# Down projection of a SwiGLU block as seven half-block products, with accumulation over two row pairs

## The chip, the core and the metric

The kernel runs on one NeuronCore of one Trainium2 chip. The metric is the device time of one execution in microseconds (us); the median of three runs before the change is 2986.15 us (2983.44 to 2987.88).

## The reference

One inference step of one decoder layer, all in float32, for a prompt of 2048 tokens and 8 decode tokens that share the weights (model width 1024). A mixer (Conformer convolution beside gated DeltaNet) with one output projection, attention into 256 memory tokens, and the dense network which the change is about:

```python
def swiglu(h, w_gate, w_up, w_down):
    return (jax.nn.silu(h @ w_gate) * (h @ w_up)) @ w_down

    x = x + y
    x = x + memory_attend(rms_norm(x, norm_mem_q), mem_k, mem_v, w_mq, w_mo)
    x = x + swiglu(rms_norm(x, norm_ffn), w_gate, w_up, w_down)
```

`w_gate` and `w_up` are 1024 x 2816, `w_down` is 2816 x 1024. A final RMS norm gives the outputs.

## The kernel before, in words

Everything is held transposed: channels on the 128 partitions, tokens along the free axis. The prompt is cut into NB = 4 blocks of TB = 512 tokens. Block 2 (`DEC_F`) carries the 8 decode tokens through the dense network, so its half blocks are 260 wide, not 256 (`width`).

**Precision.** Each float32 operand is split into a high part (a rounded float32r copy made by ScalarE) and a low part (the difference, formed on GpSimd or VectorE). `three` issues three matmuls for a product: high x high, high x low, low x high. A weight tile `w` of 128 x 2 x 512 holds both parts of four 128x128 weights. `WS` brings weights in: `load` fills a `raw` tile by DMA, `split` makes the `w` tile from it. There are NRAW = 11 raw tiles and NW = 6 weight tiles. `plan` lists them in the order of use.

**Gate and up.** The 2816 columns are NF = 22 column tiles f. For each, the two projections are computed together on half blocks of tokens in seven products, Q1, P5, P6, Q2, Q3, Q7, P4, by the Strassen-Winograd scheme: each is 4 x 3 matmuls of 256 (260) columns into one of the accumulators fx, fy, fz. Between products VectorE or ScalarE reads the accumulator and TensorE then adds the next product to it. Four of the seven weight tiles are sums of weight blocks; they are formed once (for some f in the mixer stage, for the others in block 0) and stored, split, in the DRAM tensor `sums`; later blocks load them as `w<-sums`.

**Down.** `ff_split` makes silu(gate) x up, and its two parts, for each f. Two neighbouring f are a row pair; there are NG = 11. `down(g, j)` multiplies row pair g into the two output column tiles m = 2j and 2j + 1: 2 x 2 x 3 matmuls of 512 columns (in block 2, two spans of 260 each) into a fresh PSUM bank `dn` per m. VectorE adds each bank to the residual tile `xs[m]`, and in block 2 the few decode columns into a tile `xd` of their own (`add_half`). `ffn_steps(b)` writes out the order of the steps in a block: row pair g comes in around the P4 of an even f. In block 2 the last HOLD = 3 row pairs are held back and run behind the block (`rest`), while VectorE prepares the normed operands of block 3. In block 3 `last` computes the last row pair in two spans of 256 tokens.

**Who sets the order.** The program order runs against a simple clock, in which "lanes" (generators such as `ff_split`, `ffn_norm`, `finish_x`) wait for tiles or free buffers: 28 tiles of the pool `t2`, 22 operand tiles (`act`), of which a block's normed input takes 14. All instructions are recorded on a tape; `Tape.order` then schedules the tape with a list scheduler and modelled costs and writes out the queue of every engine, TensorE's included. Each instruction therefore carries the line L469 in the profile, and is told apart by the tiles it works on. All DMAs go through the sync engine's queue. The dense networks lie at about 1290 to 1650 us (block 0), 1775 to 2130 (block 1), 2280 to 2630 (block 2), 2630 to 2965 (block 3), with the mixer's output projection and attention of blocks 2 and 3 between the first three.

Of the kernel before, what the change touches and what calls it, by code (L numbers as in the profile page):

```python
# [14 lines left out]
P = 128  # L15
# [30 lines left out]
NG = NF // 2  # L46

# [544 lines left out]
def hybrid_step(ctx: ExitStack, tc: tile.TileContext, i: dict, o: list):  # L592
# [183 lines left out]
    def ffn_steps(b):  # L776

        steps = [("Q1", 0)]
# [22 lines left out]


# [8 lines left out]
    def ffn_plan(b):  # L811
        at = {}
        for st, f, *j in ffn_steps(b):
            if st == "down":
                plan.append(("w_down", "d", f, j[0]))
            elif st == "dec":
# [70 lines left out]
    for b in range(NB):  # L887
        ffn_plan(b)
        if b + 2 < NB:
            out_plan(b + 2)  # L890
            att_plan(b + 2)
        elif b + 1 < NB:
            plan.extend(("w_down", "d", g, j) for g in range(NG - HOLD, NG) for j in range(KC // 2))
# [4 lines left out]
    class WS:  # L898
# [28 lines left out]
        def load(self):  # L927
# [4 lines left out]
            if how == "sum":  # L932
                x, y, f, k = what
                self.engine(2600.0).tensor_tensor(out=r, in0=self.raw[x], in1=self.raw[y], op=ALU.add)
                self.used(x)
                self.used(y)
            else:
                w, kind, a, b_ = what
                src = wsrc[w]
                if kind in "cd":  # L940
                    dma(r, src[a, b_], fr)
                elif kind == "q":
# [8 lines left out]
        def split(self):  # L951
# [9 lines left out]
            r = self.raw[k]  # L961
            A.activation(out=t[:, 0, :], in_=r, func=AF.Copy)
# [13 lines left out]

        def ready(self, k):
            return k < 0 or k < self.ld and C.when([self.raw[k]]) <= S.vt
# [1000 lines left out]
    wsrc["sums"] = dram.tile([NF, 4, P, 2, TB], F32, tag="sums", name="sums")  # L1979
    xpark = dram.tile([NB - 1, KC, P, TB], F32, tag="xpark", name="xpark")  # L1980
# [576 lines left out]
    def ffn_norm(b, done, op, may):  # L2557
# [10 lines left out]
        if b:  # L2568
            for k in range(KC):
                yield ("t2", 1 + RES)  # L2570
                xs[k] = t2("x")
                dma(xs[k], xpark[b - 1, k])
        if b == DEC_F:
            yield lambda: dec_lanes["f"][0] is None

# [5 lines left out]
        for k in range(4):  # L2581
            yield ("t2", 4)
            xn = []
            for kc in (k, k + 4):
                x = t2("xn", (P, 520))
                V.scalar_tensor_tensor(
                    out=halves(x, w, TB // 2), in0=halves(xs[kc], TB // 2), scalar=vcol("norm_ffn", kc),
# [38 lines left out]
    def ffn(b, op, go_on):  # L2626
# [4 lines left out]
        bank = {}  # L2631
# [13 lines left out]
        def product(st, f):  # L2645
# [31 lines left out]
            else:  # L2677
                V.tensor_tensor(out=u0, in0=pt, in1=u0, op=ALU.subtract)
                S.add(ff_split(f, u[:, : 2 * w], s_[:, : 2 * w]))
# [15 lines left out]
        def add_half(m, pts):  # L2695
            for n_, pt in enumerate(pts):
                lo, hi = n_ * TB // 2, (n_ + 1) * TB // 2
                V.tensor_tensor(out=xs[m][:, lo:hi], in0=pt[:, : TB // 2], in1=xs[m][:, lo:hi], op=ALU.add)
                if w > TB // 2:
                    dx = xd[:, m, n_ * DEC // 2 : (n_ + 1) * DEC // 2]  # L2700
                    V.tensor_tensor(out=dx, in0=pt[:, TB // 2 :], in1=dx, op=ALU.add)

        def down(g, j):
# [4 lines left out]
            for m in (2 * j, 2 * j + 1):  # L2708
                pts = [pm("dn", (P, hi - lo)) for lo, hi in spans]
                for n_, f in enumerate(fs):  # L2710
                    at = 2 * (m % 2) + n_
                    three(pts, wk(wt, 0, at), wk(wt, 1, at), hact[f], spans, n_ == 0, n_ == 1)
                    tick()
                if m % 2:
                    ws.free(1)
                if b == DEC_F:
                    add_half(m, pts)
# [7 lines left out]
        def rest():  # L2725
            for g in range(NG - HOLD, NG):
                for j in range(KC // 2):
                    down(g, j)
# [3 lines left out]
        def last():  # L2732
# [3 lines left out]
            for lo, hi in tail:  # L2736
                for m in range(KC):
                    pt = pm("dn", (P, hi - lo), ["s"])
                    for n_, f in enumerate(fs):
                        at = 2 * (m % 2) + n_  # L2740
                        three([pt], wk([wts[m // 2]], 0, at), wk([wts[m // 2]], 1, at), hact[f], [(lo, hi)], n_ == 0, n_ == 1)
# [6 lines left out]
        for st, f, *j in ffn_steps(b):  # L2748
            if st == "down":
                down(f, j[0])  # L2750
            elif st == "dec":
# [67 lines left out]
def lay_out(inp):  # L2819
# [33 lines left out]
    wd = inp["w_down"][0].reshape(NG, 2, P, KC // 2, 2, P)  # L2853
    out["w_down"] = wd.transpose(0, 3, 2, 4, 1, 5).reshape(NG, KC // 2, P, TB)
# [35 lines left out]
```

## Time and profile before

| | |
|---|---|
| median of 3 runs | 2986.15 us |
| profiled execution: time, span | 2990.62 us, 2988.8 us |
| TensorE busy, granted clock | 2932.8 us (98%), 0.994 |
| VectorE, ScalarE, GpSimd busy | 2002.1, 1312.1, 1478.9 us |
| matmuls of the down products (dn) | 2688, of these 1536 of 512 columns, 1056 of 260, 96 of 256 |
| DMA | 593.89 MB, 199 GB/s over the span |

A line of the groups reads: line, engine, operation, tile written <- tiles read, shapes, count; busy time and mean length of one; idle time of the engine just ahead of them and what ended it. Matmuls overlap, so the mean length of one is not the time that it costs; that is read from the distance of starts.

### The profile page before, as it was taken

The numbers are of one execution on the slowest core, as the hardware profiler recorded it, in microseconds if no ns is written. First come the engines' busy times: TensorE is split into PE (matmuls) and PEld (weight loads), VectorE is DVE, ScalarE is ACT, GpSimd is POOL, SyncE is SP. The second block draws the span as 40 slices with busy tenths as digits, with TensorE's granted clock in tenths as the row PEclk, the third lists the DMA queues.
The fourth block names the chain that finished last, engine by engine and source line by source line (L and its number), as shares of the span: only waits on it lengthen the run. The fifth ranks groups of instructions, "written<-read, shape, count | busy, mean of one in ns | idle before, by whom it ended". The sixth has DMA issues, their size and how long they took to land. (4 is left out here: it accounts for less than half of the span.)

```text
span 2988.8 us, 53327 instructions
## 1 busy us (share of the span) xinstructions
PE 2932.8 (98%) x18972; PEld 2609.6 (87%) x18972; DVE 2002.1 (67%) x4105; ACT 1312.1 (44%) x2672; POOL 1478.9 (49%) x1403
## 2 busy tenths in 40 slices
PE   9999999999999999999999999999999999999998
PEld 7998878887888887899988789988888999999997
DVE  8758897987755757998788974433675444664345
ACT  6533455444654344545544553333453233333233
POOL 3544554786554654457776124445413444344444
PEclk9999999999999999999999999999999999999999
DMA  6533425777663425766768767867526666666664
GB/s 213 157 102 99 138 93 173 256 236 249 222 222 117 131 82 195 234 196 212 268 252 268 247 216 244 268 220 241 185 91 227 208 226 215 212 239 220 216 224 136
DMA packets 361963, 593.89 MB, mean 199 GB/s; under 512 B 54017, under 2 KB 148545, under 8 KB 361681
## 3 DMA queue, kind: packets, MB, share of 16 engines
q1 hardware_dynamic: 361696, 590.47, 59.9%
q8 instruction: 151, 2.47, 0.3%
q14 instruction: 116, 0.94, 0.1%
HBM read 476.65 MB, written 114.27 MB: 198 GB/s over the span
## 5 line engine op out<-in xcount | busy, mean ns | idle before, releaser
L469 POOL TENSOR_TENSOR w<-raw,w 128x512 fp32r<-128x512 f32 x713 | 962.3, 1359 | 891.1 <-ACT w L469 842.3
L469 ACT ACTIVATE w<-raw 128x512 fp32r<-128x512 f32 x912 | 569.7, 631 | 905.2 <-PE fx L469 183.7
L469 PE MATMUL dn<-ff,w 128*128 128x512 f32 (+2 forms) x2688 | 518.1, 348 | 3.9 <-ACT ffs L469 2.6
L469 PEld LDWEIGHTS dn<-ff,w 128*128 128x128 f32 x2688 | 422.1, 188 | 64.7 <-ACT ffs L469 2.8
L469 PE MATMUL fy<-op,w 128*128 128x256 f32 (+1 forms) x3168 | 428.5, 283 | 4.7 <-DMA w<-sums 3.2
L469 PEld LDWEIGHTS fy<-op,w 128*128 128x128 f32 x3168 | 400.5, 189 | 10.4 <-DVE ffu L469 3.0
L469 PE MATMUL hd<-hT,w 128*128 128x512 f32 (+2 forms) x1920 | 396.7, 358 | 9.1 <-ACT w L469 5.9
L469 DVE SCALAR_TENSOR_TENSOR cacc<-cu,cw,cacc 128x512 f32<-128x512 f32 x480 | 358.2, 746 | 9.0 <-ACT cacc L469 3.8
L469 PEld LDWEIGHTS hd<-hT,w 128*128 128x128 f32 x1920 | 306.3, 190 | 54.6 <-ACT w L469 6.6
L469 DVE TENSOR_TENSOR x<-dn,x 128x512 f32<-128x512 f32 (+1 forms) x448 | 254.1, 571 | 129.2 <-PE dn L469 126.3
L469 PE MATMUL fz<-op,w 128*128 128x256 f32 (+1 forms) x2112 | 287.0, 283 | 1.0 <-DMA w<-sums 0.9
L469 PE MATMUL fx<-op,w 128*128 128x256 f32 (+1 forms) x2112 | 285.3, 283 | 1.0 <-DVE ffs L469 0.9
L469 PEld LDWEIGHTS fx<-op,w 128*128 128x128 f32 x2112 | 268.3, 189 | 7.8 <-issue 1.2
L469 PEld LDWEIGHTS fz<-op,w 128*128 128x128 f32 x2112 | 265.8, 189 | 3.7 <-issue 2.6
L469 POOL TENSOR_TENSOR sqj<-sqj,sqj 128x512 f32<-128x512 f32 (+1 forms) x98 | 134.9, 1376 | 255.7 <-ACT sqj L469 253.3
L469 DVE TENSOR_TENSOR w<-raw,w 128x512 fp32r<-128x512 f32 x199 | 167.2, 845 | 59.8 <-ACT w L469 55.8
L469 PE MATMUL sc<-w,hT 128*128 128x512 f32 x768 | 190.2, 399 | 3.2 <-DVE w L469 1.7
L469 PE MATMUL rg<-catS,w 128*128 128x512 f32 (+2 forms) x960 | 189.4, 353 | 0.0
L469 PE MATMUL rg<-pT,w 128*128 128x512 f32 x768 | 188.9, 399 | 0.4 <-ACT pT L469 0.4
L469 DVE TENSOR_TENSOR ffu<-fy,ffu 128x256 f32<-128x256 f32 (+1 forms) x176 | 74.3, 422 | 164.1 <-PE fy L469 163.7
L469 PEld LDWEIGHTS rg<-catS,w 128*128 128x128 f32 x960 | 154.4, 188 | 24.4 <-ACT jn L469 0.2
L469 PEld LDWEIGHTS sc<-w,hT 128*128 128x128 f32 x768 | 141.6, 188 | 37.5 <-DVE w L469 2.6
(378 smaller groups left out, 4089.6 us busy)
## 6 DMA issues: line engine op xcount, KB each, us to landing
w<-sums SPq DMA_DIRECT2D x296, 512.0 KB, 4.4
raw<-in_w_gate_dram SPq DMA_DIRECT2D x192, 256.0 KB, 3.2
sums<-w SPq DMA_DIRECT2D x88, 512.0 KB, 4.1
raw<-in_w_down_dram SPq DMA_DIRECT2D x176, 256.0 KB, 3.3
raw<-in_w_up_dram SPq DMA_DIRECT2D x118, 256.0 KB, 3.0
raw<-in_w_in_dram SPq DMA_DIRECT2D x96, 256.0 KB, 3.0
raw<-in_w_out_dram SPq DMA_DIRECT2D x64, 256.0 KB, 3.1
raw<-wk SPq DMA_DIRECT2D x64, 256.0 KB, 2.8
```

The lines of the kernel that those rows point to most:

```text
L469: fn(*args, **kw)
```

## The change

In blocks 1 to 3 the down products of the first 20 of the 22 column tiles f, thus of ten row pairs, are done by the same seven-product scheme. For one row pair the weight blocks are the four 128x128 blocks of two rows f and of two column tiles j and j + 4; the activations are the two rows f times the two half blocks of tokens. `downs(g, j)` takes the row pairs 2g and 2g + 1 together: each of the seven products is accumulated over both pairs (2 x 3 matmuls of 256 or 260 columns), and read by VectorE into the residual, in the order of accumulators x, y, z, x, z, x, x. The accumulators x and z go on accumulating after they have been read.

- `pair_split` replaces `ff_split` for these f: the product, four differences of half tiles on VectorE, then high and low parts in four operand tiles per row pair.
- `downs_plan`, `split_down`, `sums_down`: in block 1 the weights come as two half tiles for each row pair and j; four sums of 128x128 blocks are formed in the free halves and both tiles (512 and 384 columns) are stored unsplit in the DRAM tensor `dsums`. Blocks 2 and 3 load these. All blocks split them at each use.
- `ffn_steps_ds`: the four j of a group g stand around the P4 of two successive f (`DS_AT`). In block 2 the last group and the last row pair run in `rest`.
- The residual tiles of block 2 are 520 wide and carry the decode columns beside each half; only the last row pair writes them to `xd`.
- `down` (block 0, and the last row pair of all) takes the column tiles j and j + 4 instead of 2j and 2j + 1; the host lays `w_down` out for that.

```diff
+DS_B = 1
+NDS = 5
+
+DS_AT = ((1, 0), (1, 1), (2, 0), (2, 1))
...
+    def ffn_steps_ds(b):
...
+            units = [[], []]
+            for g in range(NDS - (b == NB - 2)):
+                for j, (df, end) in enumerate(DS_AT):
+                    if f == min(4 * g + 4 + df, NF - 1):
+                        units[end].append(("downs", g, j))
+            early = not units[0] + units[1] and f + 1 < NF
+            if early:
+                steps.append(("Q1", f + 1))
+            steps += units[0] + [("P4", f)] + units[1]
+        if b < NB - 2:
+            steps += [("down", NG - 1, j) for j in range(KC // 2)]
...
+        def sums_down(self, at, r0, r1):
+
+            (a11, a12, s1, s2), (s3, s4, a22, a21) = ([r[:, n * P : (n + 1) * P] for n in range(4)] for r in (r0, r1))
+            eng = self.engine(2600.0)
+            for out, x, y, op in (
+                (s1, a21, a22, ALU.add), (s2, s1, a11, ALU.subtract), (s3, a11, a21, ALU.subtract), (s4, a12, s2, ALU.subtract)
+            ):
+                eng.tensor_tensor(out=out, in0=x, in1=y, op=op)
+            p, j = at
+            dma(wsrc["dsums"][p, j, 0], r0)
+            dma(wsrc["dsums"][p, j, 1, :, : 3 * P], r1[:, : 3 * P])
...
+        def pair_split(p):
+
+            (u1, s1), (u2, s2) = prod.pop(2 * p), prod.pop(2 * p + 1)
+            half = lambda t, n: t[:, n * w : (n + 1) * w]
+            yield [u2, s2]
+            V.tensor_tensor(out=u2, in0=u2, in1=s2, op=ALU.mult)
+            V.tensor_tensor(out=half(s2, 1), in0=half(u2, 1), in1=half(u1, 1), op=ALU.subtract)
+            V.tensor_tensor(out=half(u1, 1), in0=half(u1, 1), in1=half(u1, 0), op=ALU.subtract)
+            V.tensor_tensor(out=half(s2, 0), in0=half(u2, 1), in1=half(u1, 1), op=ALU.subtract)
+            V.tensor_tensor(out=half(s1, 0), in0=half(u2, 0), in1=half(s2, 0), op=ALU.subtract)
+            for n, (src, wd) in enumerate(((u1, 2 * w), (u2, 2 * w), (s2, 2 * w), (s1, w))):
+                yield ("act", 1)
+                a = act("fo")
+                A.activation(out=a[:, 0, :wd], in_=src[:, :wd], func=AF.Copy)
+                yield a
+                V.tensor_tensor(out=a[:, 1, :wd], in0=src[:, :wd], in1=a[:, 0, :wd].bitcast(F32), op=ALU.subtract)
+                drop(src)
+                hx[p, n] = a
...
+        def downs(g, j):
+
+            ps_ = (2 * g, 2 * g + 1)
+            S.until(lambda: all((p, n) in hx for p in ps_ for n in range(4)), "ff")
+            wts, bk = {}, {}
+            for n, at, (x, h), t, m, half in (
+                (0, 0, (0, 0), "x", j, 0), (0, 1, (1, 0), "y", j, 0), (0, 2, (0, 1), "z", j + 4, 1), (0, 3, (2, 0), "x", j, 1),
+                (1, 1, (1, 1), "z", j, 1), (1, 0, (2, 1), "x", j + 4, 1), (1, 2, (3, 0), "x", j + 4, 0),
+            ):
+                if (n, ps_[0]) not in wts:
+                    for p in ps_:
+                        wts[n, p] = [ws.get("dsums", "s", (p, j), n)]
+                first = t not in bk
+                if first:
+                    bk[t] = pm("d" + t, (P, w))
+                pt = bk[t]
+                for p in ps_:
+                    wt = wts[n, p]
+                    three([pt], wk(wt, 0, at), wk(wt, 1, at), hx[p, x], [(h * w, (h + 1) * w)], first and p == ps_[0], p == ps_[1], True)
+                    tick()
+                if at == (3, 2)[n]:
+                    ws.free(2)
+                lo, hi = half * w, (half + 1) * w
+                V.tensor_tensor(out=xs[m][:, lo:hi], in0=pt, in1=xs[m][:, lo:hi], op=ALU.add)
+            if j == KC // 2 - 1:
+                drop(*[hx.pop((p, n)) for p in ps_ for n in range(4)])
```

More of the change, by code (lines that the diff above doesn't have):

```diff
@@ L975, in split, with split_down @@
             self.used(k)
+        def split_down(self, j, k, r, t):
+            _, _, at, n = plan[j]
+            wd = TB - n * P
+            if plan.raws[k][2] == "h" and n == 0:
+                self.sums_down(at, r, self.raw[k - 1])
+            A.activation(out=t[:, 0, :wd], in_=r[:, :wd], func=AF.Copy)
+            self.engine().tensor_tensor(out=t[:, 1, :wd], in0=r[:, :wd], in1=t[:, 0, :wd].bitcast(F32), op=ALU.subtract)
+            self.tiles[j] = t
+            self.sp += 1
+            self.used(k)
+        def sums_down(self, at, r0, r1):
[8 more added lines that the diff above has]
+            dma(wsrc["dsums"][p, j, 1, :, : 3 * P], r1[:, : 3 * P])
         def ready(self, k):
+            if 0 <= k < self.ld and plan.raws[k][2] == "h" and plan.raws[k][4] == 0 and C.when([self.raw[k - 1]]) > S.vt:
+                return False
             return k < 0 or k < self.ld and C.when([self.raw[k]]) <= S.vt
@@ L2570, in ffn_norm @@
                 yield ("t2", 1 + RES)
-                xs[k] = t2("x")
-                dma(xs[k], xpark[b - 1, k])
+                xs[k] = t2("x", (P, 2 * w))
+                dma(halves(xs[k], w, TB // 2), xpark[b - 1, k].rearrange("p (n t) -> p n t", n=2))
         if b == DEC_F:
             yield lambda: dec_lanes["f"][0] is None
+            for k in range(KC):
+                V.tensor_copy(out=halves(xs[k], w)[:, :, TB // 2 :], in_=xd[:, k, :].rearrange("p (n d) -> p n d", n=2))
         def parts_of(a, src, lo=None):
@@ L2630, in ffn, with ff_mult @@
         hact, hold = {}, {}
-        bank = {}
+        bank, prod, hx = {}, {}, {}
+        def pair_split(p):
[15 more added lines that the diff above has]
+                hx[p, n] = a
+        def ff_mult(f, u, s_):
+            yield [u, s_]
+            V.tensor_tensor(out=u, in0=u, in1=s_, op=ALU.mult)
         def ff_split(f, u, s_):
@@ L2700, in add_half @@
                     dx = xd[:, m, n_ * DEC // 2 : (n_ + 1) * DEC // 2]
[L2701 removed]
+                    V.tensor_tensor(out=dx, in0=pt[:, TB // 2 :], in1=x[:, mid:hi], op=ALU.add)
+                else:
+                    V.tensor_tensor(out=x[:, lo:hi], in0=pt, in1=x[:, lo:hi], op=ALU.add)
+            if last:
+                drop(x)
+        def downs(g, j):
[23 more added lines that the diff above has]
+                drop(*[hx.pop((p, n)) for p in ps_ for n in range(4)])
@@ L2725, in rest @@
         def rest():
-            for g in range(NG - HOLD, NG):
-                for j in range(KC // 2):
-                    down(g, j)
+            for j in range(KC // 2):
+                downs(NDS - 1, j)
+            for j in range(KC // 2):
+                down(NG - 1, j)
             if b == DEC_F:
```

80 lines of the change are left out of this document (65 added, 15 removed).

## The prediction

> **What bounds the kernel now.** I read the engine totals first, then the chain that ended last, then the engines' busy time stage by stage, then TensorE's groups by shape and its waits.
>
> ```profile
> PE 2932.8 (98%) x18972; PEld 2609.6 (87%) x18972; DVE 2002.1 (67%) x4105; ACT 1312.1 (44%) x2672; POOL 1478.9 (49%) x1403
> ...
> PEclk9999999999999999999999999999999999999999
> ```
>
> TensorE is busy for 98% of the span at full granted clock: time can only come out of its own instruction stream. The stages that the change touches, as windows (span of the stretch; PE, PEld, DVE, ACT, POOL busy; clock; DMA share; GB/s): the gated network of block 0 for comparison, then blocks 1, 2, the 30 us behind block 2 where its held-back down products run, and block 3.
>
> ```profile
> 1290.00:1640.00 350.00, 348.41 (x2429) 315.36 (x2428) 297.32 (x519) 171.03 (x344) 248.66 (x214) 1.00 0.71 240
> 1790.00:2110.00 320.00, 317.00 (x2204) 290.24 (x2203) 135.74 (x242) 111.43 (x212) 147.66 (x114) 1.00 0.74 247
> 2300.00:2595.00 295.00, 295.00 (x2454) 294.81 (x2453) 136.88 (x406) 94.08 (x181) 128.34 (x95) 1.00 0.69 224
> 2600.00:2630.00 30.00, 30.00 (x251) 29.95 (x250) 29.98 (x103) 10.76 (x18) 4.66 (x5) 1.00 0.33 110
> 2680.00:2950.00 270.00, 270.00 (x1918) 253.16 (x1917) 109.28 (x191) 83.43 (x161) 117.76 (x88) 1.00 0.67 223
> ```
>
> In blocks 1 to 3 TensorE idles about 3 us in 915, and each other engine is idle half the time. So a matmul less there is time less, as long as what replaces it doesn't make TensorE wait.
>
> **The price of a matmul.** From the chain that ended last, in block 3 (start, length, group), 12 matmuls of 256 columns in each fx, fy, fz group:
>
> ```profile
> 2915.54 8.33 PE dn L469 x36
> ...
> 2925.28 1.42 PE fz L469 x12
> ...
> 2950.75 1.44 PE fy L469 x12
> ```
>
> From 2925.28 to 2950.75 lie 18 such groups: 25.47 us / 216 = 117.9 ns per 256-column matmul. The dn row gives 8.33 / 36 = 231.4 ns per 512-column matmul; two halves cost 235.8, so halving costs 2%. In block 2 all matmuls have 260 columns:
>
> ```profile
> 2400.00:2450.00 50.00, 50.00 (x418) 49.95 (x417) 24.59 (x82) 14.31 (x27) 21.81 (x17) 1.00 0.66 210
> ```
>
> 50.00 / 418 = 119.6 ns. Here the weight loads fill the row too; as a 260-column product stays a 260-column product, that price holds after the change.
>
> **Removed and added on TensorE.** One step of the new kind (two row pairs, one pair of column tiles) replaces two old down steps. In blocks 1 and 3 the old ones are 2 x 12 = 24 matmuls of 512 columns: 24 x 231.4 = 5.55 us; the new one is 7 products x 2 pairs x 3 = 42 of 256 columns: 42 x 117.9 = 4.95 us. Gain 0.60 us. In block 2 the old ones are 48 of 260, the new one 42: 6 x 119.6 = 0.72 us. There are 5 groups x 4 = 20 steps per block: 40 x 0.60 + 20 x 0.72 = 24.1 + 14.4 = **38.4 us less**. The last row pair and all of block 0 keep their matmuls.
>
> **The new wait: an accumulator that is read and then added to.** Old down steps wrote a fresh bank each time. A new step keeps three, x, y, z, in the order x y z x z x x; VectorE adds each to the residual before TensorE may accumulate on. So z waits behind one product (6 matmuls, 0.71 us), the third x too, and the last x stands directly behind the third. Block 3's start shows what such a wait costs; PE, then VectorE:
>
> ```profile
> 2654.53 1.57 PE L469 MATMUL fz<-op,w 128*128 128x256 f32 x12
> 2656.68 1.66 PE L469 MATMUL fy<-op,w 128*128 128x256 f32 x12 [0.59 <-DVE ffu L469]
> ...
> 2661.80 0.93 PE L469 MATMUL dn<-ff,w 128*128 128x512 f32 x3 [0.61 <-DVE ffs L469]
> 2662.56 1.57 PE L469 MATMUL fy<-op,w 128*128 128x256 f32 x12
> 2663.97 0.39 PE L469 MATMUL dn<-ff,w 128*128 128x512 f32 x1
> ```
>
> ```profile
> 2656.20 0.42 DVE L469 TENSOR_TENSOR ffu<-fz,ffu 128x256 f32<-128x256 f32 x1 [0.26 <-PE fz L469]
> ```
>
> The fz group would hand over at 2654.53 + 12 x 0.1179 = 2655.94; the matmul that waited for VectorE's read starts at 2656.68: a round trip of 0.74 us when VectorE is free. A gap of 0.71 us leaves 0.03 us uncovered; a gap of none leaves 0.74. But the order written out on TensorE isn't the program's: above, 3 dn matmuls run, then 12 of fy, which the program has behind all 12 dn, then the dn go on. A list scheduler fills with whatever is ready. A step of the new kind always has a P4 or the next Q1 behind it; with 6 of those in between, the last x too is 0.03 short. That makes 3 x 0.03 x 60 = 5.4 us. VectorE is 40 to 46% busy in these rows, and an add can stand behind an operation of 0.42 to 0.88 us; the scheduler foresees most of that and fills. Ends: 0, and 0.80 x 60 = 48 us if nothing is filled. I take 6 us, near the low end, since the rows nearest (the same read-then-accumulate in the gate and up products, four times a column tile) lose almost nothing:
>
> ```profile
> L469 PE MATMUL fy<-op,w 128*128 128x256 f32 x2376 | 322.6, 284 | 3.4 <-DMA w<-sums 2.0 <-DVE ffu L469 1.0 <-DVE w L469 0.3
> L469 PE MATMUL fz<-op,w 128*128 128x256 f32 x1584 | 216.0, 283 | 0.9 <-DMA w<-sums 0.9
> L469 PE MATMUL fx<-op,w 128*128 128x256 f32 x1584 | 214.5, 283 | 1.0 <-DVE ffs L469 0.9
> ```
>
> They have a whole product (1.42 us) between, so they don't prove the tight case. The Trainium skill (Perfetto Trace Analysis, Matmuls) tells to rotate independent matmul groups through different PSUM banks so that the evacuation of one overlaps the next group; the change does the contrary at one place in seven, and by that rule alone the unfilled end of 48 us would hold. The fy group of 2662.56 between two dn groups shows the rotation restored by order, so I don't follow it to that end.
>
> **VectorE, ScalarE, GpSimd.** These rows carry the prices:
>
> ```profile
> L469 DVE TENSOR_TENSOR x<-dn,x 128x512 f32<-128x512 f32 x256 | 175.0, 687 | 98.4 <-PE dn L469 96.1
> L469 DVE TENSOR_TENSOR x<-dn,x 128x256 f32<-128x256 f32 x192 | 79.1, 417 | 30.9 <-PE dn L469 30.1
> L469 DVE TENSOR_TENSOR ff<-ffu,ff 128x512 fp32r<-128x512 f32 x66 | 57.9, 877 | 4.2 <-ACT ff L469 3.9
> L469 DVE TENSOR_TENSOR tt<-xn,tt 128x256 f32<-128x256 f32 x24 | 12.2, 510 | 0.0
> L469 DVE TENSOR_TENSOR xd<-dn,xd 128x4 f32<-128x4 f32 x176 | 25.9, 149 | 0.0
> L469 POOL TENSOR_TENSOR w<-raw,w 128x512 fp32r<-128x512 f32 x713 | 962.3, 1359 | 891.1 <-ACT w L469 842.3
> L469 POOL TENSOR_TENSOR sqj<-sqj,sqj 128x256 f32<-128x256 f32 x8 | 5.9, 741 | 8.9 <-ACT sqj L469 8.5
> L469 ACT ACTIVATE w<-raw 128x512 fp32r<-128x512 f32 x912 | 569.7, 631 | 905.2 <-PE fx L469 183.7
> ```
>
> Adds to the residual: 7 x 0.417 = 2.9 us a step for 4 x 0.687 = 2.7 before; in block 2, 2.9 for 8 x (0.417 + 0.149) = 4.5, as the decode columns now ride in the same add. Splitting the activations per row pair: four differences, 4 x 0.51, and 3.5 instead of 2 low parts, 1.5 x 0.877: 3.4 us more, 34 us a block. VectorE goes from 136 to about 173 us of 308 in block 1. I cost it at nothing: from the release of a group's eight operand tiles to the next group's first step lie 20 products, 28 us, for some 12 us of splitting. (14 of the 22 operand tiles belong to the block's normed input, so a group's 8 fill the pool and the next group's split waits for them; without that cover the split's 6 us per pair would stand on the path.)
>
> Weights: each row pair and column pair now gives a tile of 512 and one of 384 columns instead of one of 512, so ScalarE pays 40 x 0.75 x 0.631 = 19 us a block more and GpSimd 40 x 0.75 x 1.359 = 41 us. Block 1 also forms the sums: 160 operations of 128x128, some 0.37 us each (an estimate, half of the 256-column row): 59 us. GpSimd in block 1: 148 + 100 = 248 us of 308, if VectorE takes none. Block 0 carries 249 of 350 there beside 297 on VectorE, with TensorE idle 1.6 us. I cost that at nothing, too.
>
> The 30 us behind block 2: VectorE is full. The TensorE cover falls from 288 to 264 matmuls, 2.9 us; the adds fall from 48 x (0.417 + 0.149) = 27 us to 28 x 0.417 + 16 x (0.417 + 0.149) = 21 us. VectorE comes out earlier: nothing. In block 0 only the order of the column tiles changes; the norm behind it that ends later is output alone. Nothing at the kernel's end either: its last 96 matmuls and the norm keep their order.
>
> **DMA and the sync queue.** Block 1 today, window 1790 to 2110:
>
> ```profile
> DMA packets 31594, 79.05 MB, mean 247 GB/s; under 512 B 3505, under 2 KB 3505, under 8 KB 31566
> ...
> raw<-in_w_down_dram SPq DMA_DIRECT2D x40, 256.0 KB, 2.7
> ```
>
> The loads' bytes stay (as twice as many half tiles); each of 40 tiles adds stores of 256 and 192 KB: 18.4 MB. 97.4 MB in 308 us is 316 GB/s. In blocks 2 and 3 each of 40 loads becomes 448 KB: 7.9 MB more, 66 + 8 MB in 281 us, 263 GB/s. What the queues have carried with TensorE never idle:
>
> ```profile
> 1500.00:1520.00 20.00, 20.00 (x150) 17.81 (x150) 12.45 (x21) 11.49 (x23) 13.28 (x10) 1.00 0.93 339
> 2550.00:2590.00 40.00, 40.00 (x335) 40.00 (x334) 16.22 (x31) 15.11 (x31) 16.98 (x13) 1.00 0.84 289
> ```
>
> Blocks 2 and 3 are safe, costed at nothing. Block 1 lies between a rate held for 40 us and one held for 20. Each store waits in the one sync queue for its four sums (1.5 us), and the loads issued behind it wait as well; six weight tiles ahead, some 7 us, cover that. Ends: 0, and 97.4 MB at 300 GB/s = 325 us, 17 us longer. I take 3 us, near the low end, as 339 GB/s was carried and block 0 stores sums without loss. The Trainium skill (DMA: Bandwidth & Descriptors, Specifications) puts HBM traffic of a core at about 358 GB/s; by it 97.4 MB take 272 us and block 1 loses nothing. The 339 row agrees as far as it goes; the page speaks against the rival below.
>
> **Sum.** -38.4 + 6 + 3 = -29.4 us. The profiled execution took 2990.62 us (span 2988.8), 4.5 above the median of 2986.15: 2961 for it, 2957 for the median.
>
> **Rivals.**
> A. The read-then-accumulate chain eats the gain. For it: no row shows a reuse within 0.71 us that was free, and VectorE is 40 to 46% busy with other things. Against: the filled order above. It decides at 38.4 / 60 = 0.64 us per step. Unfilled, 48 us: 2986 - 38 + 48 + 3 = 2999, slower. Half of it, 24 us: 2975.
> B. Block 1 becomes bound by its supply, DMA at 300 GB/s or GpSimd late with the sums: 17 us instead of 3: 2971.
> C. All is covered: 2986 - 38.4 = 2948.
>
> **Chances.** The forecast together with C 0.72, with a range of its own of 2945 to 2967. B 0.11. A by half 0.07; A at 33 to 40 us, where nothing beyond 0.2% is left either way (6 us, about what a measurement here can tell from no change), 0.03; A in full 0.07. So faster 0.90, same 0.03, slower 0.07. The range 2945 to 2976 takes in B and A by half and leaves out the last two, 0.10, with some for the tails.
>
> **What would show it.** TensorE with 600 matmuls more (2688 dn become 768 dn and 2520 dx, dy, dz), yet busy about 30 us less; dx, dy, dz at 118 to 120 ns a matmul; idle ahead of them with VectorE named, 6 us in all right, over 20 rival A; dx groups cut by fy or fx groups where the last x waits; in block 1 idle behind the stored sums or a late weight tile, 3 us right, over 12 rival B; about 97 MB in block 1. The prediction is wrong if the half products cost over 125 ns each, or if TensorE waits at each step's end.

## The result: 18 us slower

The changed kernel takes 3006.12 us (median of 7 runs, 3000.12 to 3012.91), the kernel before 2987.88 us (7 runs on the same chip, 2983.44 to 2996.62): a ratio of 1.0053 [1.0042, 1.0064]. The profiled execution took 3008.32 us (span 3006.6). The forecast was 2957 us, its range ended at 2976.

The page of the changed kernel: engine totals and granted clock, then the groups of the gate and up products, of dx, and of the longest kind of weight transfer (columns as before: count | busy, mean ns | idle ahead of them and what ended it; the last row is a DMA issue with KB each and the median us to landing).

```profile
PE 2921.7 (97%) x19572; PEld 2629.7 (87%) x19572; DVE 2154.7 (72%) x4276; ACT 1394.5 (46%) x2852; POOL 1644.6 (55%) x1640
...
PEclk9999999999999999999999999999999999999999
...
L474 PE MATMUL fy<-op,w 128*128 128x256 f32 (+1 forms) x3168 | 436.5, 285 | 14.0 <-DMA w<-sums 10.7
...
L474 PE MATMUL fz<-op,w 128*128 128x256 f32 (+1 forms) x2112 | 293.6, 283 | 12.1 <-DMA w<-sums 11.6
L474 PE MATMUL fx<-op,w 128*128 128x256 f32 (+1 forms) x2112 | 294.8, 284 | 3.2 <-ACT ffs L474 1.8
...
L474 PE MATMUL dx<-fo,w 128*128 128x256 f32 (+1 forms) x1440 | 215.8, 286 | 0.2
...
w<-sums SPq DMA_DIRECT2D x296, 512.0 KB, 4.9
```

There are 600 matmuls more, as forecast, but TensorE is busy only 11 us less in a span 18 us longer. The new groups hardly wait (dx 0.2 us). What waits is the old work beside them: fy and fz for late weight tiles `w<-sums`, 22.3 us (11.6 and 10.7) where it was 4.1 before, in TensorE's list of waits (us in total, times, longest) of the kernel before:

```profile
PE fy L469 <- DMA w<-sums: 3.2, 4, 1.5
...
PE fz L469 <- DMA w<-sums: 0.9, 3, 0.4
```

Windows of 50 us of the changed kernel, in block 1 and behind block 2:

```profile
1850.00:1900.00 50.00, 45.78 (x350) 44.82 (x349) 29.23 (x53) 19.58 (x38) 33.25 (x38) 0.93 0.85 269
1900.00:1950.00 50.00, 46.19 (x365) 45.06 (x364) 28.45 (x58) 17.34 (x35) 33.31 (x37) 0.97 0.80 267
1950.00:2000.00 50.00, 46.23 (x368) 43.63 (x366) 27.73 (x58) 19.16 (x38) 35.02 (x44) 1.00 0.89 293
2600.00:2650.00 50.00, 47.76 (x368) 46.79 (x367) 47.48 (x110) 27.18 (x51) 22.48 (x17) 0.93 0.55 169
```

No engine is full in block 1, yet TensorE misses 4 us of each 50, and the granted clock drops in some of the windows. TensorE's timeline in the first of them shows both, and how a down step now runs (start, length, group, what it waited for; `fo` are the split activations that the new steps read, `ffu` and `ffs` the tiles in which the two projections of an f come together):

```profile
1854.73 0.99 PE L474 MATMUL fz<-op,w 128*128 128x256 f32 x7
1857.54 2.09 PE L474 MATMUL fy<-op,w 128*128 128x256 f32 x12 [1.82 <-DMA w<-sums]
1859.43 2.71 PE L474 MATMUL fx<-op,w 128*128 128x256 f32 x12
1861.97 1.59 PE L474 MATMUL fz<-op,w 128*128 128x256 f32 x12
...
1872.54 0.87 PE L474 MATMUL dy<-fo,w 128*128 128x256 f32 x6
1873.25 0.88 PE L474 MATMUL dz<-fo,w 128*128 128x256 f32 x6
1873.96 0.52 PE L474 MATMUL fx<-op,w 128*128 128x256 f32 x3
...
1874.55 0.87 PE L474 MATMUL dx<-fo,w 128*128 128x256 f32 x6
1875.26 0.87 PE L474 MATMUL dz<-fo,w 128*128 128x256 f32 x6
```

From dy at 1872.54 to dz at 1873.25 are 0.71 us for 6 matmuls, 118 ns each: the price forecast, and the median of all starts within the new groups (120 ns for 260 columns). Inside the step stand matmuls of the next gate and up products (fx at 1873.96); I call these foreign. The wait at 1857.54 is for a weight tile, and the 12 fx matmuls behind it take 1861.97 - 1859.43 = 2.54 us, 212 ns each in place of 118.

**By stage.** A stage is cut at the start of the first or last fx matmul of a block; its excess is the sum, over the matmuls in it, of the distance between starts less the full-clock pace (117.9, 119.6 or 231.4 ns by columns).

| us (excess) | block 1 and the attention behind it | block 2 and the stretch behind it | block 3 to the end |
|---|---|---|---|
| before | 504.7 (11.4) | 353.2 (4.9) | 358.2 (8.9) |
| changed | 519.5 (38.1) | 352.6 (18.9) | 357.6 (20.1) |
| length less excess, difference | -11.9 | -14.6 | -11.8 |

Together -38.3 us of matmuls and +51.9 us of waiting. The other 4.2 us between the two profiled spans stand ahead of block 1's dense part; runs of one kernel differ by up to 13 us in all, and I put no cause to them. Of the excess in the changed kernel, dx and dz have 9.4 us (in block 1 counted in its dense part alone, here and below); fy, fz, fx and the halved clock have most of the rest, and dn behind block 2 has 6 us, where it had none before.

### The profile page after: what moved, and what is told of

Its sections match the earlier page's. It is cut to its first block, busy times and chain, and to the rows that moved or that the text cites. A ratio compares the mean times of both kernels' runs of the same rounds, so it can differ in the third digit from the quotient of the medians.

```text
span 3006.6 us, 55650 instructions
## 1 busy us (share of the span) xinstructions
PE 2921.7 (97%) x19572; PEld 2629.7 (87%) x19572; DVE 2154.7 (72%) x4276; ACT 1394.5 (46%) x2852; POOL 1644.6 (55%) x1640
## 3 DMA queue, kind: packets, MB, share of 16 engines
q8 instruction: 155, 2.54, 0.3%
## 4 chain that ended last, share of the span: by engine, by line
PE 78%; DMA 9%; DVE 7%; POOL 3%; issue 2%; ACT 1%; SPq 0%; POOLq 0%; DVEq 0%; ACTq 0%
PE hd L474 11%; PE fy L474 10%; PE rg L474 10%; PE fx L474 6%; PE fz L474 6%; PE sc L474 5%; PE dx L474 4%; DMA w<-sums 4%; PE dn L474 4%; PE glua L474 3%; PE glub L474 3%; PE pu L474 2%; PE dz L474 2%; POOL w L474 2%; PE mkv L474 1%
## 5 line engine op out<-in xcount | busy, mean ns | idle before, releaser
L474 POOL TENSOR_TENSOR w<-raw,w 128x512 fp32r<-128x512 f32 (+1 forms) x794 | 1039.4, 1320 | 719.4 <-ACT w L474 628.5
L474 ACT ACTIVATE w<-raw 128x512 fp32r<-128x512 f32 (+1 forms) x1032 | 625.3, 617 | 913.7 <-PE fy L474 111.0
L474 PE MATMUL fy<-op,w 128*128 128x256 f32 (+1 forms) x3168 | 436.5, 285 | 14.0 <-DMA w<-sums 10.7
L474 DVE SCALAR_TENSOR_TENSOR cacc<-cu,cw,cacc 128x512 f32<-128x512 f32 x480 | 358.2, 746 | 9.0 <-ACT cacc L474 3.8
L474 PE MATMUL fz<-op,w 128*128 128x256 f32 (+1 forms) x2112 | 293.6, 283 | 12.1 <-DMA w<-sums 11.6
L474 PE MATMUL fx<-op,w 128*128 128x256 f32 (+1 forms) x2112 | 294.8, 284 | 3.2 <-ACT ffs L474 1.8
L474 DVE TENSOR_TENSOR w<-raw,w 128x512 fp32r<-128x512 f32 (+1 forms) x238 | 200.6, 848 | 68.6 <-ACT w L474 64.7
L474 PE MATMUL dx<-fo,w 128*128 128x256 f32 (+1 forms) x1440 | 215.8, 286 | 0.2
L474 PEld LDWEIGHTS dx<-fo,w 128*128 128x128 f32 x1440 | 187.4, 188 | 3.2 <-DVE x L474 0.7
L474 PE MATMUL dn<-ff,w 128*128 128x512 f32 (+2 forms) x768 | 174.6, 377 | 4.6 <-ACT ffs L474 2.3
```

The source lines that it names most:

```text
L474: fn(*args, **kw)
```

## The experiments

Times are medians; the ratio is to the kernel before on the same chip. The experiments ran on four chips, on which the kernel before has medians of 2987.3 to 2993.3 us, so a difference between medians of two experiments can be off by some us. Stages as in the table above, in its order, each from one profiled execution. How far a stage moves by itself e1 and e5 show: their blocks 2 and 3 do the same work, and block 2's stage takes 348.3 and 355.9 us.

### What lies behind block 1's 27 us: supply

**e1_no_sums.** Block 1 loads and splits tiles of `w_down` in the place of the sums (as blocks 2 and 3 load `dsums`; these load `w_down` too), so neither half tiles, nor sums, nor stores.

```diff
-        if b > DS_B:
+        if b >= DS_B:
...
-                    dma(r[:, :wd], src[a[0], a[1], b_, :, :wd], fr)
+                    dma(r[:, :wd], wsrc["w_down"][a[0], a[1], :, :wd], fr)
```

> Edit: block 1 forms and stores no sums; all three blocks load the 512- and 384-column weight tiles straight from w_down (so the weights are the wrong ones; everything else has the changed kernel's sizes and counts). In the trace of the changed kernel TensorE loses, beyond its matmuls' own pace, 34 us in block 1 (7 before), 12 in block 2 (3 before), 7 behind block 2 (1 before), 18 in block 3 (8 before). Theory 'sums' (the forming of the sums on GpSimd and their stores make weights late in block 1): block 1 comes down to what block 3 loses, about 16 us less, 2990 us. Theory 'slots' (a step holds 4 of the 6 weight tiles, so loads are asked for too late, in every block): block 1 keeps its loss, 3003 to 3006. Theory 'accumulators' (TensorE waits for VectorE's reads within a step): 3006, no change.

Measured 2988.68 us, 0.9985 [0.9975, 0.9994]; stages 500.5, 348.3, 354.5. Block 1 falls by 19 us: supply it is, but not yet which part.

**e5_no_store.** Half tiles are loaded and sums formed, only the stores are gone.

```diff
         def sums_down(self, at, r0, r1):
...
-            p, j = at
-            dma(wsrc["dsums"][p, j, 0], r0)
-            dma(wsrc["dsums"][p, j, 1, :, : 3 * P], r1[:, : 3 * P])
```

> Block 1 loads the halves of w_down and forms the four sums on GpSimd as in the changed kernel, but doesn't store them; blocks 2 and 3 load tiles of w_down in the place of the sums, as the run without sums did (blocks 1 to 3 are then not the reference's). Run without sums: 2988.7 us, 19 us less in block 1 and the attention behind it (519.5 to 500.5 us). If it is the extra stores (some 18 MB on the same 16 DMA engines) that make block 1's weights late, this run falls as far: 2986 to 2992 us, block 1 with what follows 500 to 504 us. If it is the forming (four GpSimd operations of 0.57 to 0.59 us to a pair of tiles, and tiles of weights that stand behind them in GpSimd's order), the time stays: 3002 to 3009 us, 515 us or more. In between: both carry it, in the ratio of the fall.

Measured 2991.89 us, 0.9995 [0.9982, 1.0007]; stages 499.7, 355.9, 356.4. Block 1 falls as far as without sums: the forming costs nothing on the path, although it is dearer than I reckoned. GpSimd's groups in the changed kernel, 1800 to 2130 us:

```profile
L474 POOL TENSOR_TENSOR raw<-raw 128x128 f32<-128x128 f32 x114 | 63.7, 567 | 30.1 <-DMA raw<-in_w_down_dram 24.8 <-issue 2.1 <-DMA dsums<-raw 1.8
...
L474 POOL TENSOR_TENSOR raw<-raw,raw 128x128 f32<-128x128 f32 x38 | 22.4, 589 | 2.8 <-DMA raw<-in_w_down_dram 2.8
```

**e7_slow_loads.** The stores stay; the list scheduler is told that a load takes longer. By its cost table it reckoned some 3.5 us for a 512 KB weight tile of the `sums` with no other load ahead (2.8 us is its figure for 256 KB), where the profile shows 4.9.

```diff
-        "dma": dict(pe=930, dve=950, act=910, pool=985, sp=930),
+        "dma": dict(pe=3430, dve=3450, act=3410, pool=3485, sp=3430),
```

> The changed kernel, one table altered: the planner that writes the order of the instructions reckons 2.5 us more from a load's issue to its use (it reckoned some 2.8 us for a weight tile of 256 KB; the traces show 4.9). Nothing else changes, and the result is the reference's. Theory: between the products of a down step the planner, which sees PE wait for VectorE's reads, pulls in products of the next rows (112 to 116 foreign matmuls inside the steps of blocks 2 and 3, none where only the last reads are left); they hold weight tiles, and with six of them the next loads are issued too late. If so, the planner that knows the loads orders this better: the waits of fy and fz for w<-sums in blocks 2 and 3 (8 to 10 us) fall to half or less, block 1's as well in part: 2990 to 3000 us. If the order isn't the cause, but the loads simply don't keep up, it stays at 3003 to 3010 us.

Measured 2990.33 us, 0.9995 [0.9983, 1.0006]; stages 503.0, 353.9, 360.3. Block 1 falls by 16.5 us with every store in place. The DMA and TensorE's waits (us in total, times, longest) from 1770 to 2130 us, first of the changed kernel:

```profile
DMA packets 50496, 101.06 MB, mean 281 GB/s; under 512 B 5536, under 2 KB 21792, under 8 KB 50456
...
w<-sums SPq DMA_DIRECT2D x86, 512.0 KB, 5.2
```

```profile
PE fy L474 <- DMA w<-sums: 9.0, 8, 2.0
PE fz L474 <- DMA w<-sums: 3.4, 3, 2.6
```

then of the run without stores:

```profile
DMA packets 42310, 88.44 MB, mean 246 GB/s; under 512 B 4602, under 2 KB 16620, under 8 KB 42270
...
w<-sums SPq DMA_DIRECT2D x87, 512.0 KB, 4.6
```

```profile
PE fy L474 <- DMA w<-sums: 3.5, 4, 2.0
```

and of this run:

```profile
DMA packets 53106, 105.36 MB, mean 293 GB/s; under 512 B 5797, under 2 KB 22949, under 8 KB 53065
...
w<-sums SPq DMA_DIRECT2D x86, 512.0 KB, 5.2
```

```profile
PE fz L474 <- DMA w<-sums: 1.0, 1, 1.0
PE fy L474 <- DMA w<-sums: 0.5, 1, 0.5
```

It moves more per second than the changed kernel, its weights land just as late after their issue (5.2 us), and the waits are gone. So the DMA's rate is not the bound. The stores lengthen a landing from 4.6 to 5.2 us and stand among the loads in the one sync queue; what these runs leave as the harm is an order that issues the loads too late for that. The wait that ended at 1857.54 in the changed kernel is an instance: its tile was asked for at 1851.10 and landed 6.3 us later. Whether the longer landing or the place in the queue weighs more, these runs don't part. In blocks 2 and 3 the expected gain did not come: the waits for `w<-sums` shrink from 9.9 to 2.9 us, and waits of fx for ScalarE (`ffu`, `ffs`: 4.8 us there, 3.8 in block 1) come in their place.

**e6_sums_early.** The sums are formed (all on GpSimd) and stored beside every second weight tile of the output and attention phases of blocks 1 and 2; block 1 then loads the finished sums besides.

```diff
+MK_AT = (("out", 1), ("att", 1), ("out", 2), ("att", 2))
+EVERY = 2
...
+            if self.on and self.mk and key[0] != "mk" and self.n % EVERY == 0:
+                at = self.mk.pop(0)
+                r1, r0 = (self.raw("dma", "w_down", "h", at, n) for n in (1, 0))
...
+                self.append(("mk", at), r0)
...
-        if b > DS_B:
+        if b >= DS_B:
```

> The reference's result. The sums are formed and stored earlier, beside every second weight tile of the output and attention phases of blocks 1 and 2 (all on GpSimd), so that block 1's dense part loads finished sums as blocks 2 and 3 do. If block 1 is slow because raw halves, sums and stores share its supply, block 1's dense part and the attention behind it fall from 519.5 to about 500 us, as without sums, and the phases that take the work over, where GpSimd and the DMA have more room, grow by 5 us or less: 2988 to 2994 us. If it is the amount of work on GpSimd and the DMA as such, wherever it stands, it only moves: 3003 to 3010 us.

Measured 3022.61 us, 1.0098 [1.0076, 1.0121]; stages 523.8, 353.3, 356.7. Block 1's dense part with the attention ahead of it takes 517.3 us, 10 less than in the changed kernel, but block 0's dense part (from its first fx to its last, 1190 to 1593 us in the changed kernel) grows from 402.5 to 427.9. Both forecasts missed: the work did not find free room; it moved, and cost more.

**e8_early_slow.** Early sums with the table of e7.

> Both at once: sums formed early, and a planner that reckons 2.5 us more for a load; the reference's result. If the two causes are separate (supply in block 1, order in blocks 2 and 3), their gains add: some 17 us and 10 us off 3006, 2976 to 2984 us, below the kernel before. If they are one (weight tiles late in the same places), the second adds nothing: no better than the better of the two alone.

Measured 3006.22 us, 1.0048 [1.003, 1.0066]; stages 519.1, 352.7, 360.9. Not additive: worse than the altered table alone by 16 us.

### What lies behind blocks 2 and 3: reads, foreign products, weight slots

**e2_slots8.** Eight weight tiles for six; the space comes from the pool `t2`.

```diff
-NW = 6
-NT2 = 28
+NW = 8
+NT2 = 24
```

> Edit: changed kernel with 8 weight tiles instead of 6, paid for with 24 instead of 28 tiles in the pool t2. Theory 'slots': TensorE's waits for w<-sums go from 22 us to under 8, in blocks 2 and 3 to near none; 15 to 22 us faster, 2984 to 2991 us. Theory 'sums': block 1 keeps most of its loss; 5 to 8 us faster, about 3000. Theory 'accumulators': no change, 3006.

Measured 3024.98 us, 1.0106 [1.0089, 1.0123]; stages 522.4, 346.2, 352.6. Block 0's dense part alone grows by 68 us for want of `t2`, so the total tells nothing. But behind block 1 the stages fall by 6 and 5 us, which alone is no more than a stage moves by itself; and in the list of TensorE's waits from 2300 to 2990 us, where the changed kernel has

```profile
PE fz L474 <- DMA w<-sums: 8.2, 10, 1.3
PE fy L474 <- DMA w<-sums: 1.7, 2, 1.2
```

no wait for `w<-sums` is left.

**e4_before_slots8.** The same two constants in the kernel before, as the control.

> Edit: the kernel before, with 8 weight tiles and 24 tiles of t2. A control for the slots. Theory 'slots': the old step holds one tile at a time and loses 4 us in all to w<-sums, so at most 4 us are to be had: 2984 to 2992 us. If it gains 10 us or more, the slots would help whatever the step is, and the second run says nothing on the new step.

Measured 3029.89 us, 1.0128 [1.0103, 1.0152]; stages 510.6, 357.6, 357.4. From block 1 on, the change gains 4.4 us with eight tiles (1221.2 to 1225.6), where it loses 13.6 with six: with the scheduler's old table, the change needs a deeper look-ahead than the kernel before.

**e3_last_reads.** VectorE reads an accumulator only after its last product, three adds a step in place of seven (which also takes 4 x 0.42 us a step off VectorE); blocks 1 to 3 are then not the reference's.

```diff
-                V.tensor_tensor(out=xs[m][:, lo:hi], in0=pt, in1=xs[m][:, lo:hi], op=ALU.add)
+                if (n, at) in ((0, 1), (1, 1), (1, 2)):
+                    V.tensor_tensor(out=xs[m][:, lo:hi], in0=pt, in1=xs[m][:, lo:hi], op=ALU.add)
```

> Edit: in each step of seven products VectorE reads only the final content of the three accumulators; the four reads between are left out, and with them TensorE's waits for them (the output lacks these four contributions). Theories 'slots' and 'sums': the excess that stands at dx and dz matmuls in the trace, 9 us, goes, the supply's waits stay: 2997 us (2995 to 3003). Theory 'accumulators', my rival A of before: most of the 52 us that TensorE lost goes: under 2975.

Measured 2984.62 us, 0.998 [0.9966, 0.9994]; stages 512.2, 341.8, 348.6. That is 21.5 us, over twice the 9.4 of dx and dz. Some 4 us of the surplus lie at dn behind block 2 (6.1 us of excess there become 1.8), where VectorE is full and each add less is time less. Most of the rest lies at fy and fz: from 2300 to 2990 us the changed kernel's 9.9 us of waits for `w<-sums` become

```profile
PE fy L474 <- DMA w<-sums: 1.6, 3, 0.9
...
PE fz L474 <- DMA w<-sums: 0.7, 3, 0.3
```

TensorE's queue suggests why. Between the first and the last dx of the 20 steps of each block stand, in blocks 1, 2, 3, 244, 141 and 124 foreign matmuls in the changed kernel's trace, and 4, 12 and 0 here. Where TensorE would wait for a read, the scheduler pulls in products of the next columns, whose weight tiles must then lie ready beside the step's own, in six slots. By this account it covers the read and leaves the next loads no slot to go out early. The account is argued, not shown: e7, whose waits for `w<-sums` shrink, has more foreign matmuls (371, 221, 256), so their number alone doesn't make the loads late.

**e9_whole_steps.** Foreign matmuls kept out of the steps by a rule in the scheduler; everything else is the changed kernel's.

```diff
+        steps, step_of, cur = {}, {}, None
...
+                if e == "pe" and cur is not None and not force:
+                    z = steps[cur][1]
+                    if any(k <= z for k, _ in avail[e]):
+                        t = clock[e]
+                    else:
+                        r = [x for x, k, _ in future[e] if k <= z]
```

> The changed kernel with one rule more for the planner: once the first product of a down step is on PE, no later matmul starts before the step's last (of the 60 steps of blocks 1 to 3, 21 are free of foreign products in the changed kernel and 55 here; matmuls, loads, sums and stores are the same; the reference's result). Theory 1, the foreign products are the harm (they hold weight tiles, and six don't last): blocks 2 and 3 fall by 7 to 8 us each, as where only the last reads were left, waits of fy and fz for w<-sums go, and the reads cost only what they cost there: 2982 to 2990 us. Theory 2, the foreign products are the cover of the reads: without them each step shows its own chain (read 0.43 us, some 0.35 us of handing over; behind the sixth product nothing lies between, behind the fourth one product of 0.71 us), 0.9 to 1.0 us to a step, 18 to 20 us to a block, on dx: blocks 2 and 3 at 318 to 324 us, 3030 to 3045 us.

Measured 3047.17 us, 1.0174 [1.0155, 1.0193]; stages 537.9, 356.5, 372.3. The second theory holds: dx alone now has 59 us of excess (20.6, 17.1, 21.5; 65 with the steps that run beside the attention behind block 1), and the wait from 1770 us on is named,

```profile
PE dx L500 <- DVE x L500: 34.2, 41, 1.8
```

(41 waits; the excess counts the short ones as well). So foreign products save more than they cost, and the bare reads are dearer than the matmuls saved. The first theory has its part: with every read in place and hardly a foreign product, the waits for `w<-sums` from 2300 to 2990 us are 2.1 us, where the changed kernel has 9.9; but TensorE is slower here, which gives the loads time as well.

**e10_whole_turns.** The same with the seven products in the order x y x z x z x.

```diff
-(0, 2, (0, 1), "z", j + 4, 1), (0, 3, (2, 0), "x", j, 1), (1, 1, (1, 1), "z", j, 1), (1, 0, (2, 1), "x", j + 4, 1),
+(0, 3, (2, 0), "x", j, 1), (0, 2, (0, 1), "z", j + 4, 1), (1, 0, (2, 1), "x", j + 4, 1), (1, 1, (1, 1), "z", j, 1),
```

> As the run with whole steps, and the seven products stand in another order: x y x z x z x instead of x y z x z x x (the accumulators' names), so that one product of another accumulator, 0.71 us, lies between any two of dx; sums, weights and reads are the same, and so is the result. If the bare reads set the pace of the whole steps, dx's waits fall to 0.1 to 0.2 us for each of three reads, 6 to 12 us to a block: 12 to 14 us less a block than the run with whole steps, 2990 to 3010 us in all. If something else sets it, the two runs agree within 5 us.

Measured 3042.43 us, 1.0163 [1.014, 1.0185]; stages 533.7, 357.6, 370.5. Inconclusive: inside a step the scheduler chose again, and 24 of the 60 steps ran as x y z x z x x.

**e13_strict_turns.** The order x y x z x z x made binding for the scheduler, in all 60 steps.

```diff
+        def allowed(k):
+            return k <= cur[-1] and (k not in follow or k == nxt)
```

> The test that the run with turns did not make: there the planner put the products of a step back into another order (24 of 60 steps ran as x y z x z x x). Here the order x y x z x z x is binding, and no foreign matmul enters (60 of 60 steps, 57 without foreign products); the reference's result. In the run with whole steps, a step that happened to go in this order took 5.19 us from its first product to the next, 0.24 us over seven times 0.71. If one product between two of dx covers the read, dx costs 60 x 0.24 = 14 us over the run with the last reads alone (2984.6): 2995 to 3004 us, 40 us less than with whole steps. If VectorE is late for other reasons (its own queue), it stays at 3030 us or more.

Measured 3037.39 us, 1.0154 [1.013, 1.0177]; stages 535.4, 357.4, 361.9. The order is not the cure: dx still has 52.5 us. Two steps of its timeline show what is. One that VectorE serves at once:

```profile
2857.18 0.88 PE L512 MATMUL dx<-fo,w 128*128 128x256 f32 x6
...
2862.38 1.58 PE L512 MATMUL fy<-op,w 128*128 128x256 f32 x12
```

5.20 us for seven products of 0.71 us, as expected; and the next:

```profile
2864.50 0.87 PE L512 MATMUL dy<-fo,w 128*128 128x256 f32 x6
2864.52 1.23 DVE L512 TENSOR_TENSOR ffu<-ffu,ffs 128x512 f32<-128x512 f32 x1
...
2865.68 0.41 DVE L512 TENSOR_TENSOR x<-dx,x 128x256 f32<-128x256 f32 x1
2866.01 0.41 DVE L512 TENSOR_TENSOR ffs<-ffu,ffu 128x256 f32<-128x256 f32 x1
...
2866.14 0.97 PE L512 MATMUL dx<-fo,w 128*128 128x256 f32 x6 [0.77 <-DVE x L512]
2866.34 0.41 DVE L512 TENSOR_TENSOR x<-dy,x 128x256 f32<-128x256 f32 x1
2866.68 0.41 DVE L512 TENSOR_TENSOR ffu<-ffu 128x256 f32<-128x256 f32 x1
```

The multiplication of `pair_split` (from 2864.52) has started before the read of dx, and a difference (at 2866.01) before the read of dy, and VectorE works in its order. A read of 0.41 us behind an operation of 1.23 is late however the products stand.

**e14_strict_slow.** e13 with the table of e7.

> The same, and the planner that reckons 2.5 us more for a load, which alone took 17 us off block 1 and 5 us off what stands ahead of it (it lets 97 to 108 foreign matmuls a block in again, as it holds back the loads); the reference's result. If the two gains are separate: 2976 to 2988 us, at or below the kernel before with that planner (2985.7). If the planner's gain in block 1 came from the foreign products themselves, it is gone: 2992 to 3004 us.

Measured 3026.58 us, 1.0121 [1.0098, 1.0143]; stages 526.5, 357.2, 366.3; both of its forecasts missed, since dx keeps its 52.8 us. The table's gain in block 1 is half of what it was (9 us).

**e11_turns_slow.** The order x y x z x z x, not binding, with the table of e7.

> The order x y x z x z x and the planner that reckons 2.5 us more for a load, without the rule of whole steps; the reference's result. The planner alone gave 2990 us with dx's waits at 3 to 5 us a block. If these are the accumulator's, they halve: 2983 to 2988 us. If they are DVE's own queue, no change: 2989 to 2992 us.

Measured 2990.17 us, 0.9994 [0.9984, 1.0003]; stages 502.1, 354.4, 360.9. No change against e7, as forecast for VectorE's own queue; but not binding, the order was again the scheduler's (by the trace some 12 of the 60 steps ran as x y x z x z x), so this run adds little to e13.

### Does the account close?

**e12_before_slow.** The table of e7 in the kernel before.

> The kernel before with the planner that reckons 2.5 us more for a load. It has waits of 8.1, 4.6 and 3.4 us over the matmuls' pace in its three dense parts and none of the new steps: if the planner's error costs only where the look-ahead is short, it stays within 4 us of before, 2986 to 2994 us. If the altered planner is better everywhere (the stages ahead of block 1 took 5 us less in the changed kernel), 2978 to 2986 us, and then the change loses against it as it did.

Measured 2985.65 us, 0.997 [0.9958, 0.9982]; stages 504.1, 351.4, 355.3. Of the kernels that compute everything, the fastest is the one before with a truer table, 0.3% faster than before; the changed kernel with that table (e7, ratio 0.9995) loses to it by 0.25%, some 7 us.

**e15_last_slow.** Last reads only (e3) and the table of e7.

> Only the last read of each output tile is left (each accumulator is added to the residual once, so blocks 1 to 3 aren't the reference's), and the planner that reckons 2.5 us more for a load. The two causes as named so far, the reads in between with what they let in, and loads ordered too late in block 1, are both gone. If they are all of the loss, the forecast of 2957 us comes back within 15 us: 2960 to 2972 us (blocks 2 and 3 as with the last reads, 303 and 300 us, block 1 with the attention behind it at 500). If a third cause is left, such as traffic in block 1, it stays at 2978 us or more.

Measured 2967.05 us, 0.9921 [0.9899, 0.9942]; stages 497.5, 343.0, 350.3.

**e16_no_store_last.** Last reads only (e3), no stores (e5), the old table.

> The last reads alone and no stores of the sums in block 1 (and tiles of w_down in the place of the sums in blocks 2 and 3), the planner as it was; blocks 1 to 3 aren't the reference's. No stores took 13 us off the profiled span, last reads 24. If they are two causes, the sum: 2966 to 2972 us. If the stores' harm came only through foreign products that hold weight tiles, the stores cost nothing where these are gone: 2980 to 2985 us.

Measured 2971.17 us, 0.993 [0.9909, 0.9951]; stages 497.4, 341.2, 349.5. In both runs the two causes add: the reads are worth 22 us with either table, the stores' lateness 13 to 18 with either kind of reads.

## Why the prediction was wrong, point by point

- **The matmuls, -38.4 us: right.** A half product starts 118 ns after the last (120 for 260 columns), and at that pace the new counts make -38.3 us in the table, in the three blocks as forecast (-12.0, -14.4, -12.0). Length less excess is counts times pace by its definition, so the pace is what was measured.
- **The accumulators, +6 us: mis-sized, and the mechanism only half seen.** I forecast that the scheduler would fill the gaps and let filling be free. It filled, and dx and dz kept 9.4 us; but the reads in all cost 22 us (e3 against the changed kernel 21.5, e15 against e7 23.3), some 4 of it at dn behind block 2, and most of the rest as weight tiles late at fy and fz. That the filling takes their slots fits e2, e3 and e9, and e7 shows that it is not the filling alone. The bound of 48 us for unfilled reads was too low as well: 59 us (e9), for I priced a read on a free VectorE. The rule of the Trainium skill that I weighed and did not follow (Perfetto Trace Analysis, Matmuls: rotate independent groups through the banks) speaks of that bare case, and e9 agrees with it.
- **"I cost it at nothing" for `pair_split`: wrong where it meets the reads.** I asked whether VectorE has the time (it has) and not what stands ahead of a read in its queue. In the changed kernel the difference `ffs<-ffu,ffu`, for which I reckoned 0.51 us, takes 0.90 in the mean (window 2700 to 2950):

```profile
L474 DVE TENSOR_TENSOR ffs<-ffu,ffu 128x256 f32<-128x256 f32 x17 | 15.3, 900 | 0.1
```

  The mean hides two kinds. Of those that start in the window eight take 0.41 us, with GpSimd idle, and eight take 1.40 to 1.52, each beside a running operation of GpSimd:

```profile
2843.97 0.41 DVE L474 TENSOR_TENSOR ffs<-ffu,ffu 128x256 f32<-128x256 f32 x1
...
2845.57 1.29 POOL L474 TENSOR_TENSOR w<-raw,w 128x512 fp32r<-128x512 f32 x1 [2.40 <-DMA w<-sums]
2845.64 1.51 DVE L474 TENSOR_TENSOR ffs<-ffu,ffu 128x256 f32<-128x256 f32 x1
```

  So the long ones, which make the queue that the reads stand in longer, coincide with GpSimd's work on the weights; no run takes that work away to test it.
- **Block 1's supply, +3 us: the step that failed first.** "Six weight tiles ahead, some 7 us, cover that": in the order that the scheduler wrote they do not. A step uses four weight tiles, the first two of them free again only after its fourth product, and a tile of the `sums` lands 5.2 us after its issue. With the altered table the same six slots do cover it (e7). The stores cost 14 us by e5, 16 by e7's order. I had looked for a rate. The 14 to 16 us lie inside my bounds of 0 and 17, but the rate did not bind (293 GB/s in e7 without loss). On this the Trainium skill's figure (DMA: Bandwidth & Descriptors, Specifications) was no contradiction, and no guard: about 358 GB/s says nothing of when a tile lands.
- **GpSimd's sums, 59 us estimated, nothing on the path: price wrong, verdict right.** They took 0.57 to 0.59 us each, not 0.37, and cost nothing (e5).
- **Blocks 2 and 3 "safe", and nothing behind block 2: wrong** by the 14 and 11 us of excess in the table. The waits for weight tiles go with eight slots (e2) or without the reads between (e3). But 6 of the 18.9 us in block 2's stage are dn's behind the block: I had VectorE come out earlier there, and it is busy for 47.48 of 50 us in the window shown, TensorE waits for its adds and splits (2.3 us), and the clock drops (0.93).
- **The rivals.** A was the nearest, but through weight tiles at fy and fz, and with 0.2 us idle at dx where I had asked for 20; B was named with 17 us at most. Each alone ends at 2999 or below; both came. The terms as measured make -38 + 22 + 15, and with the 20 us that follow next 19, where 18 was measured.
- **What stays open.** With both causes gone, e15 is 18.6 us faster than e12 (medians on two chips; the profiled spans differ by 19.5) and not 38.4. The other 20 us are excess again, 5, 6 and 7 us in the three stages, at fx behind ScalarE, at fy and at the last row pair behind block 2. I did not test them.

## What to carry to other kernels

When an accumulator is read and then added to, price the read from the queue that it stands in, not from the engine's mean load, and price the cover too: work pulled in holds buffers that something else needed. Count how many slots of a look-ahead one step occupies; with four of six in use, a transfer of 5 us comes onto the path as soon as the order asks for it late, however free the DMA is. A scheduler's table is worth checking against the landing times of the trace: one row of it was worth more here than the change.

## What the runs showed of the hardware that I had not expected

- A stall of about 2 us can halve TensorE's pace for the 3 us behind it: start to start 0.118 us before, then 212 ns a matmul from 1859.43 to 1861.97, behind a gap from 1855.56 (1854.73 + 7 x 0.118) to 1857.54. The same stands behind the next long wait:

```profile
1879.85 0.40 PE L474 MATMUL fz<-op,w 128*128 128x256 f32 x2
1882.21 2.77 PE L474 MATMUL fy<-op,w 128*128 128x256 f32 x12 [1.96 <-DMA w<-sums]
1884.78 0.63 PE L474 MATMUL fx<-op,w 128*128 128x256 f32 x2
```

  These are 12 matmuls in 2.57 us, 214 ns each. Such stretches cost 6.0 us in block 1; in the kernel before there was none between 1274 and 2980 us. Not every such stall does it. In the run without stores (e5) 12 matmuls behind one of 1.99 us take 1947.79 - 1946.28 = 1.51 us, 126 ns each, and the granted clock from 1940 to 1960 is 1.00:

```profile
1946.28 1.68 PE L474 MATMUL fy<-op,w 128*128 128x256 f32 x12 [1.99 <-DMA w<-sums]
1947.79 1.59 PE L474 MATMUL fx<-op,w 128*128 128x256 f32 x12
```

  What tells the two kinds of stall apart, no run here tests. The Trainium skill (TensorE: Matmul & The Clock Gate, Part 1) has the clock halved after at least one idle window of about 3.4 us; here 2.0 us of idling had the same effect in some places, and the measurement decides.
- GpSimd's price fell by less than the size: 567 ns in the mean for 128 columns (median 464, least 442), where half of the 741 ns for 256 was expected.
